# A low weight part of each up unit made by an accumulating transfer instead of VectorE, and the conditioning tiles dealt anew

## The chip, the core and the metric

The kernel runs on one core of a Trainium2 chip. A core has TensorE (PE in the profile; PEld is its weight load), VectorE (DVE), ScalarE (ACT), GpSimd (POOL) and SyncE (SP), which run their own instruction queues in order and wait for one another by semaphores, and 16 DMA engines that move data between the chip's memory and the tiles. The metric is the time of one execution in microseconds of device time. A ratio is time before over time after.

## The reference

A decoder trunk of four layers over 256 tokens of width 1024, in float32. The conditioning vector `c` gives six vectors of 1024 for each layer; each layer has a token mixer (layer 0 and 3: gMLP; 1: latent attention, MLA; 2: HGRN2) and a feed-forward part with a short convolution:

```python
for i in range(DEPTH):
    mod = c_act @ ada_w[i] + ada_b[i]
    sh1, sc1, g1, sh2, sc2, g2 = jnp.split(mod, 6, axis=-1)
    h = modulate(rmsnorm(x, mix_norm_g[i]), sh1, sc1)
    ...
    x = x + (1.0 + g1)[:, None, :] * y
    h = modulate(rmsnorm(x, ffn_norm_g[i]), sh2, sc2)
    x = x + (1.0 + g2)[:, None, :] * conv_ffn(h, ff_w_up[i], ff_conv_w[i], ff_conv_b[i], ff_w_down[i])
return rmsnorm(x, final_g)
```

`ada_w` is 4 x 1024 x 6144, `ff_w_up` 4 x 1024 x 5632 and `ff_w_down` 4 x 2816 x 1024. All of them are read once.

## The kernel before

**Weights in two parts.** Every product is made in a faster format that holds fewer bits (fp32r): a weight is split into a high part (the weight rounded to that format) and a low part (what is left), and so is the activation; three matmuls (high by high, high by low, low by high) replace one. The weights arrive in *units* of 128 x 2048 (1 MB) in a tile `raw`, of which there are five. A unit has two halves of 1024 columns. For each half, `conv_half` has ScalarE cast the high part `wh` (L214) and VectorE subtract it from `raw` to make the low part `wl` (L217); seven tiles of each go round. So 209 units give 418 casts and 418 subtractions.

**The order of units.** `want` writes all units into the list `plan` in the order of use. `unit` is called where a unit is used; it issues loads on SP's queue for units ahead (`dma_next`, L190) and converts units ahead, two or three beyond the one in use, then calls `pacing`.

**Stages.** In each layer: the mixer (gMLP: v, u and the output product go; MLA: cq, ckv, q, kn, heads, wo; HGRN2: hf, hq, hi, hg, o, wo), then the 22 units of the up projection (`ffn`: 48 matmuls a unit, then convolution and gate on ScalarE and VectorE, L1318 to L1325) and the 11 units of the down projection (dn). Between two stages stands a joint: `out_end` adds the product to `x` in pieces (L541, L542; the first piece is named `early` and is placed behind the last subtraction issued so far), forms the mean square, scales (`gx`, L477 to L481), and `modulated` turns `gx` by TensorE (`xt`, L489) and writes the next stage's activations in two parts (`hh`, `hlo`).

**Conditioning.** The 24 vectors of 1024 are the *conditioning units* (layer, part); the first two are made at the start. Each of the others has four tiles of 1 MB (named `adaw_part_tile`). Those in the list `ADA_P` are multiplied by TensorE (L331, into `adaps`; SP loads them at L317), those in `ADA_D` by VectorE (L356, two instructions of 1024 columns a tile; loaded at L347). Tables of numbers deal them out: `RATE` says how many tiles of each kind a unit of a stage loads, `GAPS` and `GAPRUN` how many TensorE tiles are held for and run in each of the joints, `MLA_ADA` and `HGF` at which places of MLA and HGRN2 one runs. Parts 2 and 5 are gates of the residual: `gate_row` clears a small tile `gcol` on GpSimd (L273), turns it on VectorE and stores it, and `gate_load` reads it back as `gx` (L293).

GpSimd has little else to do: fills, two broadcasts and a mask in each gMLP, and two products at the end.

Of the kernel before, what the change touches and what calls it, by code (L numbers as in the profile page):

```python
# [8 lines left out]
F32 = mybir.dt.float32  # L9
# [4 lines left out]
ALU = mybir.AluOpType  # L14
# [6 lines left out]
L = 4  # L21
# [3 lines left out]
NF = 22  # L25
GI = 2048
NRAW = 5
GAPS = [2, 4, 3, 3, 1, 2, 2, 0]
GAPRUN = [2, 2, 3, 3, 1, 2, 2]
GAPW = 7  # L30
GAPBIG = 3
LAST = 3
# [9 lines left out]
OLAG = 1  # L42
ROPE = 1
MLA_ADA = (2, 4, 6)
HGF = 2
HGO = "o0 o1 s0 a0 o2 s1 a1 n0 o3 s2 n1 w0 s3 n2 w1 n3 w2 w3"
HOLD = (3, 4)
ADA_P = [(0, 5), (1, 2), (1, 3), (2, 2), (2, 3), (2, 4), (3, 5)]
ADA_D = [(0, 2), (0, 3), (0, 4), (1, 0), (1, 1), (1, 4), (1, 5), (2, 0), (2, 1), (2, 5), (3, 0), (3, 1), (3, 2), (3, 3),
         (3, 4)]  # L50
RATE = {("mix", 0): (0.05, 0.9), ("u", 0): (0.1, 0.8), ("go", 0): (0.35, 0.6), ("up", 0): (0.1, 0.23),
        ("dn", 0): (0.0, 0.65), ("mix", 1): (2.0, 0.0), ("up", 1): (0.0, 0.2), ("dn", 1): (0.0, 0.85),
        ("mix", 2): (0.0, 0.0), ("lev", 2): (0.5, 0.0), ("hout", 2): (0.25, 0.0), ("up", 2): (0.0, 0.2),
        ("dn", 2): (0.0, 0.8), ("mix", 3): (0.0, 0.6), ("u", 3): (0.0, 0.5), ("go", 3): (0.0, 0.7),
        ("up", 3): (0.0, 0.0), ("dn", 3): (0.0, 0.0)}
MAGIC = 12582912.0
TWO_PI = 2.0 * math.pi
# [35 lines left out]
def build(ctx, tc, A, out, stages=None):  # L93
    nc = tc.nc
    pe, act, dve, pool = nc.tensor, nc.scalar, nc.vector, nc.gpsimd
# [60 lines left out]
    i = act.activation(cact[:], cin[:], AF.Silu)  # L156
# [12 lines left out]

    plan = []  # L170

    def want(aps):
        plan.extend(aps)

    state = {"dma": 0, "conv": 0, "use": 0, "ahead": 3, "chain": (), "behind": (), "manual": False, "left": 99, "tag": "raw", "p": 0.0, "d": 0.0, "gap": 0, "rate": {"p": 0.0, "d": 0.0}}
    raws = []
# [1 line left out]
    halves = []  # L178

    def dma_next():  # L180
        ap, n = plan[state["dma"]]
        raw = wp.tile([P, 2048], F32, tag="raw", name=f"raw{state['dma']}", bufs=NRAW)
        state["dma"] += 1
        if state["dma"] == 1:

            nc.sync.dma_start(raw[:, :1024], ap[:, :1024])
            raw_, ap = raw[:, 1024:], ap[:, 1024:]
        else:
            raw_ = raw[:, :n]
        i = nc.sync.dma_start(raw_, ap)  # L190
        state["lastdma"] = getattr(i, "ins", i)
        raws.append((raw, n))

    def conv_half():

        if not halves:
            if state["dma"] == state["conv"]:
                if state["dma"] == len(plan):
                    return
                dma_next()  # L200
            raw, n = raws.pop(0)
            ready.append([])
            halves.extend((raw, o, min(1024, n - o), state["conv"]) for o in range(0, n, 1024))
            state["conv"] += 1
        raw, o, w, n = halves.pop(0)
        wh = wp.tile([P, 1024], F32R, tag="wh", name=f"wh{n}_{o}", bufs=7)
        wl = wp.tile([P, 1024], F32R, tag="wl", name=f"wl{n}_{o}", bufs=7)
        with contextlib.ExitStack() as es:

            for ins in state["chain"]:  # L210
                es.enter_context(tc.issue_after(ins))
            if n == 0 and o and "first" in state:
                es.enter_context(tc.issue_after(state["first"][1]))
            act.copy(wh[:, :w], raw[:, o : o + w])  # L214
            if n == 0 and "first" in state:
                es.enter_context(tc.issue_after(state["first"][0]))
            i = dve.tensor_tensor(wl[:, :w], raw[:, o : o + w], wh[:, :w].bitcast(F32), op=ALU.subtract)  # L217
            state["sub"] = getattr(i, "ins", i)
        ready[-1].append((wh, wl))

    def unit(ahead=None, more=DMA_AHEAD):
# [11 lines left out]
    def pace(kind, l, left=None, tag=None):  # L233
        state["rate"] = dict(zip("pd", RATE[kind, l]))
        state["gap"] = GAPS[2 * l + (kind in ("up", "dn"))]
        if left is not None:
            state["left"] = left
        if tag is not None:
            state["tag"] = tag
# [67 lines left out]
    def ada_tile(name, shape):  # L307
        if state["tag"] == "big":
            return big(name, shape)
        return wp.tile(list(shape), F32, tag="raw", name=name, bufs=NRAW)  # L310

    def ada_tensor(l, u):


        def load(i):
            raw = ada_tile(f"adaw{l}_{u}_{i}", (P, 2, 4, 256))
            nc.sync.dma_start(raw[:].rearrange("p a b c -> p (a b c)"), A["adap"][ADA_P.index((l, u)), i])  # L317

            def run():
                h = ADA_P.index((l, u)) % 2  # L320
                ps = adaps[:, h, :]
                if i == 0 and pend[h] in late:
                    late.remove(pend[h])
                    pend[h][1]()
                with contextlib.ExitStack() as es:
                    for ins in state["behind"]:
                        es.enter_context(tc.issue_after(ins))
                    for k in range(2):
                        kc = 2 * i + k
                        for j in range(4):  # L330
                            pe.matmul(ps[32 * j : 32 * j + 32, :], crep(kc), raw[:, k, j, :], start=kc == 0, stop=kc == KC - 1,  # L331
                                      tile_position=(0, 32 * j))
                if i == 3:
                    pend[h] = (state["use"], lambda: mod_store(l, 8 * u, 8, ps), (l, u))
                    late.append(pend[h])
# [5 lines left out]
    def ada_vector(l, u):  # L341
# [3 lines left out]
        def load(i):  # L345
            raw = ada_tile(f"adaw{l}_{u}_{i}", (P, 2, D))
            nc.sync.dma_start(raw[:].rearrange("p a b -> p (a b)"), A["adad"][ADA_D.index((l, u)), i])  # L347

# [55 lines left out]
    def ada_run(m):  # L404
        if not loaded[m]:
            ada_load(m)
        if loaded[m]:
            loaded[m].pop(0)[1]()
            owner[m].pop(0)
# [57 lines left out]
    def root(t, sd):  # L467

        i = dve.reciprocal(sd[:, t : t + 1], sd[:, t : t + 1])
        state["chain"] = (getattr(i, "ins", i),)  # L470
        return sd[:, t : t + 1]

    def scaled(t, rs):

        xn = cur["gx"][:, t, :]
        if t == 0:
            dve.tensor_scalar_mul(xn, x[:, t, :], rs)  # L477
            return
        for o in (0, 256):
            dve.tensor_scalar_mul(xn[:, o : o + 256], x[:, t, o : o + 256], rs)  # L480
        i = act.activation(xn[:, 512:D], x[:, t, 512:D], AF.Copy, scale=rs)  # L481
        state["chain"] += (getattr(i, "ins", i),)
# [35 lines left out]
    def modulated(l, which):  # L518
# [4 lines left out]
        state["behind"] = (state["mm"],)  # L523
        for _ in loaded["p"][: GAPRUN[2 * l + which - 1]]:
            ada_run("p")
# [241 lines left out]
    def gmlp_units(j):  # L767
        want([(A["gmv"][j, i], 2048) for i in range(8)])
        want([(A["gmu"][j, i], 2048) for i in range(8)])
        want([(A["gmo"][j, i], 2048) for i in range(8)])  # L770
# [340 lines left out]
    def hgrn(l):  # L1111
# [176 lines left out]
        for step in HGO.split():  # L1288
            {"o": recur, "s": root, "n": normed, "w": wo.step, "a": lambda i: ada_run("p") if i < HGF else None}[step[0]](int(step[1]))

# [7 lines left out]
            nc.sync.dma_start(convs[l][:], A["cwb"][l])  # L1298

    def ffn_units(l):  # L1300
        want([(A["up"][l, i], 2048) for i in range(NF)])
        want([(A["dn"][l, i], 2048) for i in range(NF // 2)])

    def ffn(l):
        gh, gl = hilo("g", NF)
# [33 lines left out]
    for kind, l in stages:  # L1339
        if kind == "mix":  # L1340
            if l % 3 == 0:
                gmlp_units(l // 3)
            elif l == 1:
                mla_units()
            else:
                hg_units()
        elif kind == "ffn":
            ffn_units(l)
# [19 lines left out]
    for t in range(2):  # L1368
        act.activation(ss0[:, 6 + t : 7 + t], ss0[:, t : t + 1], AF.Sqrt, bias=epsc[:], scale=1.0 / D)
        scaled(t, root(t, ss0[:, 6:8]))  # L1370
    for m, units in (("p", ADA_P), ("d", ADA_D)):
        for l, u in units:
# [61 lines left out]
def pack(i):  # L1434
# [23 lines left out]
    def rng(a, n):  # L1458
# [12 lines left out]
    ap = aw.reshape(L, 4, 2, P, 6, 8, 4, 32)  # L1471
    r["adap"] = np.stack([ap[l, :, :, :, u].transpose(0, 2, 1, 4, 3, 5).reshape(4, P, 2048) for l, u in ADA_P])

    r["adad"] = np.stack([np.ascontiguousarray(aw[l, :, u * D : u * D + D].T).reshape(4, 2, P, D).transpose(0, 2, 1, 3).reshape(4, P, 2048)
                          for l, u in ADA_D])
    r["cb"] = np.ascontiguousarray(np.broadcast_to(f["c"], (P, D)))
# [48 lines left out]
```

## Time and profile before

| | |
|---|---|
| median of three runs (lowest, highest) | 1356.22 us (1356.13, 1357.68) |
| the profiled execution, its own time | 1358.56 us |
| its span in the profile | 1356.8 us |
| mean granted clock of TensorE | 0.991 |
| busy: TensorE, VectorE, ScalarE, GpSimd | 1320.5, 1129.1, 782.9, 20.0 us |
| moved by the DMA engines | 330.71 MB, mean 244 GB/s |

A line of a timeline has the start, the duration, the engine, the line of the kernel, the operation, what it writes and reads by the program's names, and in brackets how long the engine stood idle before it and what ended that. A line of a group has the count, the busy time and the mean in ns, then the idle time before its members. Matmuls overlap, so the time from one start to the next tells what one costs.

### The profile page before, as it was taken

What the parts mean: (1) busy time and instruction counts of PE and PEld (TensorE: products, weight loads), DVE (VectorE), ACT (ScalarE), POOL (GpSimd) and SP (SyncE); (2) the same over time, 40 slices, a digit from 0 to 9 for tenths busy, and PEclk for the clock granted to TensorE, in tenths of its full rate; (3) what the DMA queues carried; (4) which work ended last, traced back from release to release, by engine and by line L of the source; (5) the groups of instructions that cost most, each with busy time, mean ns of one, the idle gap of its engine ahead of it and who ended that gap; (6) DMA issues with size and microseconds to landing.
All of it is one profiled execution on the core that took longest, in us unless ns stands there. A gap on an engine that the chain in (4) does not pass through costs nothing. (4 is left out here: it accounts for less than half of the span.)

```text
span 1356.8 us, 25080 instructions
## 1 busy us (share of the span) xinstructions
PE 1320.5 (97%) x10197; PEld 1200.1 (88%) x10197; DVE 1129.1 (83%) x1865; ACT 782.9 (58%) x1230; POOL 20.0 (1%) x29
## 2 busy tenths in 40 slices
PE   9999999999979999999999999999999999999997
PEld 7799889997768799997897979999778998999986
DVE  5699979889776679999978967899988896888874
ACT  4664466665266566654585547666455753766642
POOL 0100000000000000000010000000001000000000
PEclk9999999999989999999999999999999999999999
DMA  9978955666985355579665364567968588355550
GB/s 380 357 266 312 397 205 214 257 218 232 394 325 203 125 187 202 200 303 372 249 221 199 109 261 156 187 217 280 372 255 338 198 326 330 122 172 178 198 198 32
DMA packets 49308, 330.71 MB, mean 244 GB/s; under 512 B 6565, under 2 KB 7717, under 8 KB 10407
## 3 DMA queue, kind: packets, MB, share of 16 engines
q1 hardware_dynamic: 48032, 326.95, 64.3%
q10 hardware_dynamic: 1160, 2.17, 0.5%
q8 instruction: 80, 1.31, 0.4%
q14 instruction: 36, 0.29, 0.1%
HBM read 328.01 MB, written 1.08 MB: 243 GB/s over the span
## 5 line engine op out<-in xcount | busy, mean ns | idle before, releaser
L214 ACT CAST wh<-raw 128x1024 fp32r<-128x1024 f32 x418 | 428.9, 1050 | 324.2 <-PE up L700 94.5
L217 DVE TENSOR_TENSOR wl<-raw,wh 128x1024 fp32r<-128x1024 f32 x418 | 506.9, 1231 | 93.4 <-ACT wh L214 88.7
L699 PE MATMUL up<-hh,wh 128*128 128x256 f32 x1280 | 314.3, 283 | 0.0
L700 PE MATMUL up<-hlo,wh 128*128 128x256 f32 x1280 | 314.1, 283 | 0.0
L699 PEld LDWEIGHTS up<-hh,wh 128*128 128x128 f32 x1280 | 245.7, 192 | 0.8 <-ACT gh L647 0.4
L700 PEld LDWEIGHTS up<-hlo,wh 128*128 128x128 f32 x1280 | 245.7, 192 | 0.0
L703 PE MATMUL up<-hh,wl 128*128 128x256 f32 x1280 | 179.7, 283 | 0.0
L703 PEld LDWEIGHTS up<-hh,wl 128*128 128x128 f32 x1280 | 165.1, 192 | 0.0
L356 DVE CUSTOM_DVE_ANT_0 adaw<-adaw,cbc,prm 128x1024 f32<-128x1024 f32 x120 | 151.3, 1280 | 3.9 <-DMA adaw<-adad 3.8
L1318 ACT ACTIVATE y<-up,cwb 128x256 f32<-128x256 f32 x176 | 98.8, 562 | 69.6 <-DVE y L1320 69.6
L248 PE MATMUL dn<-wl,gh 128*128 128x512 f32 x339 | 133.5, 394 | 1.5 <-DVE wl L217 1.5
L247 PE MATMUL dn<-wh,gh 128*128 128x512 f32 x339 | 130.2, 390 | 4.1 <-DVE y L1320 2.7
L249 PE MATMUL dn<-wh,gl 128*128 128x512 f32 x339 | 131.2, 390 | 0.0
L1319 DVE SCALAR_TENSOR_TENSOR y<-up,cwb,y 128x255 f32<-128x255 f32 x176 | 84.5, 480 | 29.8 <-ACT y L1318 29.0
L1320 DVE SCALAR_TENSOR_TENSOR y<-up,cwb,y 128x254 f32<-128x254 f32 x176 | 84.2, 478 | 1.8
L247 PEld LDWEIGHTS dn<-wh,gh 128*128 128x128 f32 x339 | 63.7, 188 | 18.5 <-ACT warm L624 3.5
L248 PEld LDWEIGHTS dn<-wl,gh 128*128 128x128 f32 x339 | 63.6, 188 | 18.4 <-DVE wl L217 5.7
L249 PEld LDWEIGHTS dn<-wh,gl 128*128 128x128 f32 x339 | 63.6, 188 | 12.8
L699 PE MATMUL u<-hh,wh 128*128 128x256 f32 x256 | 64.6, 290 | 0.0
L700 PE MATMUL u<-hlo,wh 128*128 128x256 f32 x256 | 62.8, 283 | 0.0
L648 DVE TENSOR_TENSOR gl<-g,gh 128x256 fp32r<-128x256 f32 x88 | 37.1, 421 | 19.3 <-ACT gh L647 18.0
L552 ACT ACTIVATE gated<-x 128x512 f32<-128x512 f32 (+1 forms) x40 | 21.8, 545 | 52.9 <-DVE x L542 50.4
(383 smaller groups left out, 2234.6 us busy)
## 6 DMA issues: line engine op xcount, KB each, us to landing
raw<-up SPq DMA_DIRECT2D x88, 1024.0 KB
adaw<-adad SPq DMA_DIRECT2D x60, 1024.0 KB
raw<-dn SPq DMA_DIRECT2D x44, 1024.0 KB
adaw<-adap SPq DMA_DIRECT2D x28, 1024.0 KB
raw<-gmu SPq DMA_DIRECT2D x16, 1024.0 KB
raw<-gmo SPq DMA_DIRECT2D x16, 1024.0 KB
raw<-gmv SPq DMA_DIRECT2D x15, 1024.0 KB
adaf<-ada SPq DMA_DIRECT2D x7, 1024.0 KB
```

The source lines that it names most:

```text
L214: act.copy(wh[:, :w], raw[:, o : o + w])
L217: i = dve.tensor_tensor(wl[:, :w], raw[:, o : o + w], wh[:, :w].bitcast(F32), op=ALU.subtract)
L247: pe.matmul(ps, lh, rh, start=start, stop=False)
L248: pe.matmul(ps, lh, rl, start=False, stop=False)
L249: i = pe.matmul(ps, ll, rh, start=False, stop=stop)
L356: r = dve.tensor_tensor_reduce(raw[:, e, :], raw[:, e, :], cbc[:], 1.0, prm[:, c0 : c0 + 1], ALU.mult, ALU.add, mod[:, l, b : b + 1])
L699: pe.matmul(ps[:, g, :], a, src_h(k), start=k == 0, stop=False)
L700: pe.matmul(ps[:, g, :], a, src_l(k), start=False, stop=False)
L703: i = pe.matmul(ps[:, g, :], b, src_h(k), start=False, stop=k == nk - 1)
L1318: act.activation(y[:], ps[:, e, :], AF.Identity, bias=b, scale=w[2])
L1319: dve.scalar_tensor_tensor(y[:, 1:], ps[:, e, : S - 1], w[1], y[:, 1:], op0=ALU.mult, op1=ALU.add)
L1320: dve.scalar_tensor_tensor(y[:, 2:], ps[:, e, : S - 2], w[0], y[:, 2:], op0=ALU.mult, op1=ALU.add)
```

## The change

`want` marks the units of which the first half is to be made in another way: all 22 up units and the first three dn units of each layer. For such a half ScalarE writes the negated, rounded weight into `wl` (`act.mul` by -1, which rounds as the cast does), and a transfer issued from GpSimd adds the weight from memory onto it, so that `wl` becomes the same difference. These bytes are read from memory a second time. The conditioning units are dealt anew: TensorE has six of them (24 tiles) where it had seven (28), VectorE 16 (64 tiles) where it had 15 (60); unit (0, 5) goes to VectorE, and the rates differ.

```diff
-GAPS = [2, 4, 3, 3, 1, 2, 2, 0]
-GAPRUN = [2, 2, 3, 3, 1, 2, 2]
+GAPS = [2, 4, 3, 3, 2, 2, 2, 0]
+GAPRUN = [2, 2, 3, 3, 2, 2, 2]
...
-HGF = 2
+HGF = 1
...
-ADA_P = [(0, 5), (1, 2), (1, 3), (2, 2), (2, 3), (2, 4), (3, 5)]
+ADA_P = [(1, 2), (1, 3), (1, 4), (2, 3), (2, 4), (3, 5)]
...
-RATE = {("mix", 0): (0.05, 0.9), ("u", 0): (0.1, 0.8), ("go", 0): (0.35, 0.6), ("up", 0): (0.1, 0.23),
-        ("dn", 0): (0.0, 0.65), ("mix", 1): (2.0, 0.0), ("up", 1): (0.0, 0.2), ("dn", 1): (0.0, 0.85),
+RATE = {("mix", 0): (0.05, 0.9), ("u", 0): (0.1, 0.85), ("go", 0): (0.35, 0.4), ("up", 0): (0.0, 0.34),
+        ("dn", 0): (0.0, 0.5), ("mix", 1): (2.0, 0.0), ("up", 1): (0.0, 0.36), ("dn", 1): (0.0, 0.9),
...
-    def want(aps):
-        plan.extend(aps)
+    def want(aps, again=0):
+
+        plan.extend((*a, i < again) for i, a in enumerate(aps))
...
+        again = plan[n][2] and o == 0
...
-            i = dve.tensor_tensor(wl[:, :w], raw[:, o : o + w], wh[:, :w].bitcast(F32), op=ALU.subtract)
-            state["sub"] = getattr(i, "ins", i)
+            if again:
+
+                act.mul(wl[:, :w], raw[:, o : o + w], -1.0)
+                pool.dma_start(wl[:, :w], plan[n][0][:, o : o + w], accum_op=ALU.add)
+            else:
+                i = dve.tensor_tensor(wl[:, :w], raw[:, o : o + w], wh[:, :w].bitcast(F32), op=ALU.subtract)
+                state["sub"] = getattr(i, "ins", i)
...
-        want([(A["up"][l, i], 2048) for i in range(NF)])
-        want([(A["dn"][l, i], 2048) for i in range(NF // 2)])
+        want([(A["up"][l, i], 2048) for i in range(NF)], NF)
+        want([(A["dn"][l, i], 2048) for i in range(NF // 2)], 3)
```

ScalarE's queue just before the joint into layer 0's up stage, where the first two up units are converted (`raw_1753` and `raw_1777` before, `raw_1751` and `raw_1773` now; the number in `wh_` or `wl_` is the half's first column). Before:

```order
L214 CAST wh_0_1781<-raw_1753 128x1024
L214 CAST wh_1024_1785<-raw_1753 128x1024
L214 CAST wh_0_1789<-raw_1777 128x1024
L214 CAST wh_1024_1793<-raw_1777 128x1024
L552 ACTIVATE gated,ss<-x 128x512 x2
```

And with the change:

```order
L215 CAST wh_0_1777<-raw_1751 128x1024
L220 ACTIVATE wl_0_1778<-raw_1751 128x1024
L215 CAST wh_1024_1782<-raw_1751 128x1024
L215 CAST wh_0_1786<-raw_1773 128x1024
L220 ACTIVATE wl_0_1787<-raw_1773 128x1024
L215 CAST wh_1024_1791<-raw_1773 128x1024
L558 ACTIVATE gated,ss<-x 128x512 x2
```

A copy of 1024 columns now stands between the casts of a unit's two halves, and VectorE's subtraction of the second half, behind which `early` is placed, waits for the second cast.

SP's queue in the second half of layer 0's down stage, from the load of the gate to the first units of MLA (`adad` are VectorE's conditioning tiles, `adap` TensorE's). Before:

```order
L293 DMA gx<-gate_3381 128x1024
L190 DMA raw_3843<-dn 128x2048
L190 DMA raw_3881<-dn 128x2048
L317 DMA adaw_2_3_3893<-adap 128x2048
L347 DMA adaw_1_2_3628<-adad 128x2048
L347 DMA adaw_1_3_3700<-adad 128x2048
L347 DMA adaw_4_0_3736<-adad 128x2048
L317 DMA adaw_2_0_3775<-adap 128x2048
L347 DMA adaw_4_1_3813<-adad 128x2048
L317 DMA adaw_2_1_3815<-adap 128x2048
L347 DMA adaw_4_2_3853<-adad 128x2048
L317 DMA adaw_2_2_3855<-adap 128x2048
```

Behind these came one dn unit, `adaw_4_3_3931` and the two units of mla_a. With the change, from the same place:

```order
L299 DMA gx<-gate_2865 128x1024
L190 DMA raw_3848<-dn 128x2048
L353 DMA adaw_1_0_3672<-adad 128x2048
L353 DMA adaw_1_1_3744<-adad 128x2048
L323 DMA adaw_2_2_3780<-adap 128x2048
L353 DMA adaw_1_2_3818<-adad 128x2048
L323 DMA adaw_2_3_3820<-adap 128x2048
L323 DMA adaw_3_0_3858<-adap 128x2048
L190 DMA raw_3884<-dn 128x2048
L353 DMA adaw_1_3_3896<-adad 128x2048
L323 DMA adaw_3_1_3898<-adap 128x2048
```

Behind these come one dn unit and the two units of mla_a: 13 tiles of 1 MB from the load of the gate on, where there were 15.

More of the change, by code (lines that the diff above doesn't have):

```diff
@@ L44 @@
 MLA_ADA = (2, 4, 6)
-HGF = 2
+HGF = 1
 HGO = "o0 o1 s0 a0 o2 s1 a1 n0 o3 s2 n1 w0 s3 n2 w1 n3 w2 w3"
 HOLD = (3, 4)
-ADA_P = [(0, 5), (1, 2), (1, 3), (2, 2), (2, 3), (2, 4), (3, 5)]
-ADA_D = [(0, 2), (0, 3), (0, 4), (1, 0), (1, 1), (1, 4), (1, 5), (2, 0), (2, 1), (2, 5), (3, 0), (3, 1), (3, 2), (3, 3),
-         (3, 4)]
-RATE = {("mix", 0): (0.05, 0.9), ("u", 0): (0.1, 0.8), ("go", 0): (0.35, 0.6), ("up", 0): (0.1, 0.23),
-        ("dn", 0): (0.0, 0.65), ("mix", 1): (2.0, 0.0), ("up", 1): (0.0, 0.2), ("dn", 1): (0.0, 0.85),
-        ("mix", 2): (0.0, 0.0), ("lev", 2): (0.5, 0.0), ("hout", 2): (0.25, 0.0), ("up", 2): (0.0, 0.2),
-        ("dn", 2): (0.0, 0.8), ("mix", 3): (0.0, 0.6), ("u", 3): (0.0, 0.5), ("go", 3): (0.0, 0.7),
+ADA_P = [(1, 2), (1, 3), (1, 4), (2, 3), (2, 4), (3, 5)]
+ADA_D = [(l, u) for l in range(L) for u in range(6) if (l, u) > (0, 1) and (l, u) not in ADA_P]
+RATE = {("mix", 0): (0.05, 0.9), ("u", 0): (0.1, 0.85), ("go", 0): (0.35, 0.4), ("up", 0): (0.0, 0.34),
+        ("dn", 0): (0.0, 0.5), ("mix", 1): (2.0, 0.0), ("up", 1): (0.0, 0.36), ("dn", 1): (0.0, 0.9),
+        ("mix", 2): (0.0, 0.0), ("lev", 2): (0.5, 0.0), ("hout", 2): (0.0, 0.0), ("up", 2): (0.0, 0.36),
+        ("dn", 2): (0.0, 0.6), ("mix", 3): (0.0, 0.5), ("u", 3): (0.0, 0.5), ("go", 3): (0.0, 0.5),
         ("up", 3): (0.0, 0.0), ("dn", 3): (0.0, 0.0)}
@@ L180, in dma_next @@
     def dma_next():
-        ap, n = plan[state["dma"]]
+        ap, n, _ = plan[state["dma"]]
         raw = wp.tile([P, 2048], F32, tag="raw", name=f"raw{state['dma']}", bufs=NRAW)
```

## The prediction

> **What bounds the kernel now.** I read the page's head, then stretches by stage, then the timeline at the joints between stages.
>
> ```profile
> span 1356.8 us, 25080 instructions
> PE 1320.5 (97%) x10197; PEld 1200.1 (88%) x10197; DVE 1129.1 (83%) x1865; ACT 782.9 (58%) x1230; POOL 20.0 (1%) x29
> ...
> L214 ACT CAST wh<-raw 128x1024 fp32r<-128x1024 f32 x418 | 428.9, 1050 | 324.2 <-PE up L700 94.5
> L217 DVE TENSOR_TENSOR wl<-raw,wh 128x1024 fp32r<-128x1024 f32 x418 | 506.9, 1231 | 93.4 <-ACT wh L214 88.7
> ...
> L356 DVE CUSTOM_DVE_ANT_0 adaw<-adaw,cbc,prm 128x1024 f32<-128x1024 f32 x120 | 151.3, 1280 | 3.9 <-DMA adaw<-adad 3.8
> ```
>
> PE is at work nearly always, so an engine that gets less to do gives time back only where PE stands. The stretches show where that is (the columns are the stretch, its length, busy us of PE, PEld, DVE, ACT and POOL, granted clock, DMA share, GB/s). The first row is the down projection of layer 0, the next the up projection of layer 1, then the down projection of layer 1 and the up projection of layer 3.
>
> ```profile
> 307.50:370.00 62.50, 59.59 (x258) 47.54 (x257) 53.13 (x85) 25.87 (x33) 0.00 (x0) 1.00 0.83 328
> 475.00:601.70 126.70, 126.70 (x1059) 126.70 (x1057) 110.96 (x191) 82.36 (x131) 0.26 (x2) 1.00 0.61 222
> 601.70:662.00 60.30, 58.94 (x259) 47.72 (x259) 56.93 (x81) 25.33 (x33) 0.00 (x0) 1.00 0.92 363
> ...
> 1162.00:1288.00 126.00, 126.00 (x1053) 126.00 (x1052) 103.93 (x180) 82.46 (x133) 0.12 (x1) 1.00 0.50 172
> ```
>
> **An up stage is PE alone**: 126.70 of 126.70 us, while DVE has 110.96 (88%) and ACT 82.36 (65%). Nothing that relieves DVE there shortens it. What can be won lies at the joints, and the worst one stands between the down projection of layer 0 and layer 1's attention:
>
> ```profile
> 361.75 1.99 ACT L214 CAST wh<-raw 128x1024 fp32r<-128x1024 f32 x2 [16.14 <-DMA raw<-dn]
> 366.70 2.00 ACT L214 CAST wh<-raw 128x1024 fp32r<-128x1024 f32 x2 [2.96 <-DMA raw<-mla_a]
> 367.79 4.80 DVE L217 TENSOR_TENSOR wl<-raw,wh 128x1024 fp32r<-128x1024 f32 x4
> 369.14 2.00 ACT L214 CAST wh<-raw 128x1024 fp32r<-128x1024 f32 x2 [0.44 <-DMA raw<-mla_a]
> 372.50 0.68 DVE L541 TENSOR_TENSOR early<-dn,gx 128x512 f32<-128x512 f32 x1
> 381.06 3.71 PE L489 MATMUL xt<-ident,gx 128*128 128x128 f32 x16 [6.94 <-DVE gx L477]
> 384.42 0.56 PE L687 MATMUL cq<-hh,wh 128*128 128x256 f32 x1
> ```
>
> ACT waits 16.14 us for the last tiles of dn, then for those of mla_a; DVE makes their low parts, and only behind these stands the residual ("early", 372.50), from which the chain to the next transposes takes 8.56 us. PE has ended its tail by then. So the joint hangs on the transfers, and they are saturated:
>
> ```profile
> 171.40:174.90 3.50, 0.35 (x9) 0.09 (x2) 3.25 (x11) 2.34 (x9) 0.00 (x0) 1.00 0.94 393
> 373.70:381.00 7.30, 0.41 (x8) 0.00 (x0) 6.82 (x17) 4.73 (x13) 0.00 (x0) 0.71 1.01 425
> 381.00:388.00 7.00, 6.94 (x36) 6.75 (x36) 6.06 (x17) 6.64 (x12) 0.00 (x0) 0.57 0.96 386
> 741.70:744.20 2.50, 0.21 (x27) 0.11 (x13) 2.50 (x4) 1.72 (x2) 0.00 (x0) 1.00 0.18 26
> 744.20:749.00 4.80, 4.80 (x80) 4.11 (x80) 4.69 (x6) 0.00 (x0) 0.00 (x0) 0.64 0.90 323
> ```
>
> 425 GB/s at a full share is the most that the engines move here. PE idles for 7.30 us, and in the 7.00 us after it the granted clock is 0.57. The joint into layer 0's up stage (first row) is a smaller case of the same.
>
> **The change, part by part.** *The low parts.* 100 halves (22 up units and 3 dn units in each of four layers) leave L217: 100 x 1.231 = 123 us off DVE. ACT gets 100 scaled copies; the row nearest is its cast of the same shape, so 100 x 1.05 = 105 us. One DVE unit of conditioning is added, 8 x 1.28 = 10 us. In the stretch of layer 1's up stage DVE goes from 110.96 by -21 x 1.23 and, with four tiles more, +8 x 1.28 to about 95 of 126.7; ACT from 82.36 by +22 x 1.05 to about 105 (83%). Neither becomes the bound, and PE stays where it is: **0 us in the up stages**. PE's 5.76 us a unit hide it (126.7/22), with units converted two ahead, so a low part may land some 11 us after its copy. If that cover is gone, each unit is late by what the slowest engine exceeds 5.76 us.
>
> *The accumulating transfer* is in no row of before. Bounds: below, it costs its 0.52 MB at 420 GB/s, 1.25 us of all engines; above, that its bytes are read from memory, read from the tile and written back, three times as much, 3.75 us. Layer 1's up stage moves 222 x 126.7 = 28.1 MB now; the four tiles more make 32.3, and engines at 420 GB/s could move 53.2. So 20.9 MB, or 0.95 MB for each of 22 accumulates, is free: they are hidden up to 2.26 us apiece, 1.8 times the plain price. I take 1.25 to 2.2 us, nearest to the only rows there are, plain loads, and hence nothing for it. On GpSimd's queue stand behind such a transfer the next one and the fills of "gcol" (eight in all, on whose landing DVE waits); each waits for ACT's copy at most, and DVE's own next subtraction is behind the same copies, so I cost them at 0, at most 1 us each.
>
> The Trainium skill, *DMA: Bandwidth & Descriptors* (Specifications), puts the limit of memory to one core near 358 GB/s. By that, accumulates would be hidden only up to about 1.4 us (an estimate). The trace disagrees, with its 425 GB/s.
>
> *Layer 0's down stage.* On SP's queue, from the load of gx to the second tile of mla_a, stand 15 tiles of 1 MB before and 13 now, two conditioning tiles fewer. At 425 GB/s a tile is 2.5 us: the chain from 366.70 on starts 5.0 us earlier. What is late next is DVE's chain itself, which begins then at 367.5, before the tail ends. PE's 7.30 us of idling fall to about 2.3, and with them the slow clock: 0.43 x 7.00 = 3.0 us, of which I take 2.5, since ACT and DVE are busy there too. Together **-7.5 us**; at worst the room is filled by other transfers, 0. In the stage itself PE idles 62.50 - 59.59 = 2.91 us against 60.30 - 58.94 = 1.36 in layer 1's, because of the same late tiles: **-1.5 us** (0 at worst).
>
> *Conditioning tiles on PE* go from 28 to 24. Two stood in layer 0's up stage:
>
> ```profile
> 223.78 0.88 PE L703 MATMUL up<-hh,wl 128*128 128x256 f32 x6
> 224.59 1.07 PE L331 MATMUL adaps<-adaw,cact 128*32 128x256 f32 x16
> 225.59 0.39 PE L699 MATMUL up<-hh,wh 128*128 128x256 f32 x1
> ```
>
> The next up matmul would have started 0.72 us after 223.78 and starts at 225.59: 1.09 us a tile, **-2.2 us**. One fewer stands in HGRN, where PE also waits for others: **-0.5 us** (0 to -1.1). Two are gone from the joint into layer 3's up stage, where nothing else fills PE:
>
> ```profile
> 1157.18 0.28 PE L249 MATMUL tail<-wh,yl 128*128 128x256 f32 x1
> 1157.39 1.93 PE L331 MATMUL adaps<-adaw,cact 128*32 128x256 f32 x32
> 1159.84 0.63 PE L489 MATMUL xt<-ident,gx 128*128 128x128 f32 x4 [0.52 <-DVE ss L469]
> ```
>
> PE stands there 2.5 us now. After the 2.50 us at 741.70 the clock was 0.64 for 4.80 us, 1.7 us lost; so 0 to +1.7, and I take **+0.9 us**. The Trainium skill, *TensorE: Matmul & The Clock Gate* (Part 1), has the clock halved after an idle window of about 3.4 us; by it this term is 0. The row at 741.70 differs.
>
> *Layer 1's down stage* gets one tile more on SP's queue (2.5 us) and three accumulates (3.75 us) into a stretch whose engines have 8% of 60.30 us free, 4.8 us: **+1.5 us** at its joint (0 to +5).
>
> *The joint into layer 0's up stage:*
>
> ```profile
> 163.09 2.00 ACT L214 CAST wh<-raw 128x1024 fp32r<-128x1024 f32 x2 [0.42 <-DMA raw<-up]
> ...
> 166.46 0.68 DVE L541 TENSOR_TENSOR early<-go,gx 128x512 f32<-128x512 f32 x1
> ```
>
> One tile less makes the last up tile land 2.5 us earlier; the accumulate of the unit ahead takes 1.25 of it back, and the scaled copy that stands before the second cast 1.05. Sum **-0.2 us**; bounds -4 (all DVE waits gone and the clock kept) and +2.3 (the accumulate at its upper price).
>
> Sum: -7.5 - 1.5 - 2.2 - 0.5 + 0.9 + 1.5 - 0.2 = **-9.5 us**. The profiled execution took 1358.56 us, 1.8 more than its span; it becomes 1349.1. The median of the three runs is 1356.22, 2.3 under it, so I forecast 1356.2 - 9.5 = **1347 us**.
>
> **Rivals.** *The transfers become the bound of the up stages* (slower). It decides from 2.26 us an accumulate. At 3.1 us, the middle of the range above that, each of the 66 units of layers 0 to 2 is 0.84 us late, +55 us, and layer 3, at 172 GB/s now, has room for it: 1356 + 55 - 9 = 1402; just past the point, at 2.45 us, it is +12, and the time is 1359. For it speaks that such a transfer must read its target as well; against it, that all four stages show 0.50 to 0.61 of the engines used.
>
> *The room in layer 0's down stage is filled* (no change): the accumulates of the three dn units and what the up stage left over take the two tiles' place. Then only the tiles on PE count, -2.7 + 2.4, and the time is about 1356. The full share at 373.70 speaks for it; against it, that ACT's 16.14 us of waiting begin long after these three units.
>
> *DVE's relief is worth more*: SP's loads also wait for buffers that DVE's subtractions free, so with less behind DVE the down stages begin with more loaded, and the joint into layer 0's up stage gains its 4 us too: 1340.
>
> That the change doesn't do what it says would show as DVE's L217 group still at 418; the order of instructions excludes that.
>
> **How the numbers follow.** Forecast (with the sum's own bounds, 1343 to 1353) 0.45; more relief, 0.25; no change, 0.12; transfers bound, 0.18. A measurement of this kernel can tell about 0.2%, 2.7 us, from no change. Faster takes the first two cases, 0.70; same 0.12; slower 0.18. The range from 1336 to 1366 holds the first three and the mild end of the last; left out are the fully bound up stages and a gain beyond 20 us.
>
> **What would show it.** Right: the stretch of layer 1's up stage still 126.7 us with PE busy throughout, DMA share between 0.8 and 1.0; "early" in layer 0's down stage at least 4 us ahead of the tail's end and the granted clock 1.00 after it; no tiles inside layer 0's up stage. Wrong: PE waiting for low parts made by GpSimd's transfer inside an up stage, a DMA share of 1.0 there, or ACT above 95% of such a stretch. If "early" still waits for tiles of mla_a, the main term has failed.

## The result and the profile after

The changed kernel takes **1371.69 us** (median of five runs, 1366.64 us the lowest), and the kernel before, run five times beside it, 1357.68 us. Every ratio from here on is time after over time before, so that a number above 1 means slower: 1.0094, with a 95% interval of 1.0072 to 1.0116. One of the five runs took 1823.44 us, at a granted clock of 0.654 where the others had 0.988 to 0.993, and is left out of the ratio; the median of the other four is 1370.57 us. The forecast was 1347 us with a range of 1336 to 1366. The change makes the kernel about 0.9% slower, and both the sign and the range were wrong.

The page of the changed kernel (its profiled execution took 1369.45 us), first the head, the queue that GpSimd issues to (packets, MB, share of 16 engines' span), then the groups:

```profile
span 1367.7 us, 25279 instructions
PE 1315.2 (96%) x10133; PEld 1196.8 (88%) x10133; DVE 1038.8 (76%) x1779; ACT 870.8 (64%) x1330; POOL 111.3 (8%) x129
...
q0 software_dynamic: 14400, 52.44, 19.8%
...
L223 DVE TENSOR_TENSOR wl<-raw,wh 128x1024 fp32r<-128x1024 f32 x318 | 388.2, 1236 | 130.8 <-ACT wh L215 130.1
...
L709 PE MATMUL up<-hh,wl 128*128 128x256 f32 x1280 | 180.8, 284 | 9.9 <-DMA wl<-up 9.9
L362 DVE CUSTOM_DVE_ANT_0 adaw<-adaw,cbc,prm 128x1024 f32<-128x1024 f32 x128 | 164.0, 1292 | 20.3 <-DMA adaw<-adad 20.3
...
L253 PE MATMUL dn<-wh,gh 128*128 128x512 f32 x339 | 134.0, 395 | 13.9 <-DVE y L1326 13.9
...
L220 ACT ACTIVATE wl<-raw 128x1024 fp32r<-128x1024 f32 x100 | 105.5, 1055 | 5.8 <-PE wo L254 2.9
...
wl<-up POOLq DMA_DIRECT2D x88, 512.0 KB, 10.4
```

The change does what it says: the subtractions fall from 418 to 318, and DVE is 90 us less busy. PE's own work is 5 us less too. Still the span is 10.9 us longer, so PE waits more. One wait is new, PE's 9.9 us for low parts made by GpSimd's transfers. Two have grown: DVE's for conditioning tiles to 20.3 us (3.9 before) and PE's in the down stages, for "y" from DVE, to 13.9 us. The row of before for the latter has 2.7:

```profile
L247 PE MATMUL dn<-wh,gh 128*128 128x512 f32 x339 | 130.2, 390 | 4.1 <-DVE y L1320 2.7
```

The first row to read is q0's. The packets of its 100 transfers took 19.8% of 16 engines over 1367.7 us, so **one accumulating transfer takes 0.198 x 1367.7 / 100 = 2.71 us of all engines** for 0.52 MB. The break-even in the prediction was 2.26 us.

The stretches of the changed kernel, with the columns of the prediction's rows (stretch, length, busy us of PE, PEld, DVE, ACT, POOL, granted clock, DMA share, GB/s): the joint behind layer 0's down stage and what follows it, then layer 1's up stage, its down stage, and the start of that down stage.

```profile
464.20:595.30 131.10, 127.18 (x1052) 126.24 (x1051) 96.84 (x184) 99.91 (x154) 18.39 (x22) 1.00 0.97 293
595.30:660.20 64.90, 59.50 (x259) 48.94 (x259) 56.56 (x81) 29.01 (x36) 1.74 (x2) 0.97 1.01 405
```

```profile
370.80:373.30 2.50, 0.42 (x9) 0.03 (x1) 2.14 (x8) 2.04 (x9) 0.00 (x0) 1.00 1.01 426
373.30:380.00 6.70, 6.68 (x56) 6.44 (x56) 5.92 (x16) 6.62 (x12) 0.12 (x1) 1.00 1.01 428
...
604.40:612.00 7.60, 7.60 (x27) 6.13 (x28) 7.60 (x15) 2.77 (x5) 0.00 (x0) 0.79 1.03 332
```

In layer 1's up stage the DMA engines are full (0.97, before 0.61) although only 293 GB/s are moved. The bytes of an accumulating transfer are counted once (52.44 MB for 100), and the engines work on it for longer. At the joint behind layer 0's down stage the intended gain is there: PE idles 2.45 us instead of 7.30, and the granted clock stays at 1.00 where it had been 0.57. The timeline of the changed kernel shows where that gain is lost again, at the end of layer 1's up stage:

```profile
588.83 1.28 DVE L362 CUSTOM_DVE_ANT_0 adaw<-adaw,cbc,prm 128x1024 f32<-128x1024 f32 x1 [5.90 <-DMA adaw<-adad]
...
590.55 0.56 ACT L1324 ACTIVATE y<-up,cwb 128x256 f32<-128x256 f32 x1 [7.26 <-DVE y L1326]
...
598.61 0.39 PE L255 MATMUL dn<-wh,gl 128*128 128x512 f32 x1
604.40 0.77 PE L253 MATMUL dn<-wh,gh 128*128 128x512 f32 x1 [5.40 <-DVE y L1326]
```

DVE stands 5.90 us for a conditioning tile that comes late through the full engines. Behind it in DVE's queue stands the convolution of the up stage's last units, ACT stands 7.26 us for that, and PE, which has run out of activations, stands from 598.61 to 604.40 in the down stage, after which the clock is 0.79 for 7.60 us. Layer 2 repeats it, in another stretch of the same timeline, with PE standing for 6.79 us from 952.66 on:

```profile
943.61 1.28 DVE L362 CUSTOM_DVE_ANT_0 adaw<-adaw,cbc,prm 128x1024 f32<-128x1024 f32 x1 [6.80 <-DMA adaw<-adad]
```

So a good part of the loss is not where the transfer itself is waited for, but one engine and one stage further on.

### The profile page after: what moved, and what is told of

It reads as the page before. It is cut to its first block, busy times and chain, and to the rows that moved or that the text cites. A ratio compares the mean times of both kernels' runs of the same rounds, so it can differ in the third digit from the quotient of the medians.

```text
span 1367.7 us, 25279 instructions
## 1 busy us (share of the span) xinstructions
PE 1315.2 (96%) x10133; PEld 1196.8 (88%) x10133; DVE 1038.8 (76%) x1779; ACT 870.8 (64%) x1330; POOL 111.3 (8%) x129
## 3 DMA queue, kind: packets, MB, share of 16 engines
q0 software_dynamic: 14400, 52.44, 19.8%
## 4 chain that ended last, share of the span: by engine, by line
PE 55%; DVE 17%; DMA 13%; issue 7%; ACT 6%; POOL 0%; SPq 0%; ACTq 0%; DVEq 0%; POOLq 0%
PE dn L253 5%; PE dn L255 4%; PE dn L254 4%; PE up L709 4%; PE up L706 4%; PE up L705 4%; DVE wl L223 4%; DVE adaw L362 4%; DMA adaw<-adad 3%; DMA wl<-up 3%; ACT wh L215 2%; DMA raw<-dn 2%; PE v L750 2%; DMA adaf<-ada 1%; DVE x L548 1%
## 5 line engine op out<-in xcount | busy, mean ns | idle before, releaser
L223 DVE TENSOR_TENSOR wl<-raw,wh 128x1024 fp32r<-128x1024 f32 x318 | 388.2, 1236 | 130.8 <-ACT wh L215 130.1
L362 DVE CUSTOM_DVE_ANT_0 adaw<-adaw,cbc,prm 128x1024 f32<-128x1024 f32 x128 | 164.0, 1292 | 20.3 <-DMA adaw<-adad 20.3
L709 PEld LDWEIGHTS up<-hh,wl 128*128 128x128 f32 x1280 | 164.9, 192 | 12.3 <-DMA wl<-up 12.2
L253 PE MATMUL dn<-wh,gh 128*128 128x512 f32 x339 | 134.0, 395 | 13.9 <-DVE y L1326 13.9
L221 POOL DMA_DIRECT2D wl<-up x88 | 76.8, 873 | 767.5 <-ACT wl L220 407.3
L220 ACT ACTIVATE wl<-raw 128x1024 fp32r<-128x1024 f32 x100 | 105.5, 1055 | 5.8 <-PE wo L254 2.9
## 6 DMA issues: line engine op xcount, KB each, us to landing
wl<-up POOLq DMA_DIRECT2D x88, 512.0 KB, 10.4
```

What stands on the lines that cost most here:

```text
L220: act.mul(wl[:, :w], raw[:, o : o + w], -1.0)
L253: pe.matmul(ps, lh, rh, start=start, stop=False)
L362: r = dve.tensor_tensor_reduce(raw[:, e, :], raw[:, e, :], cbc[:], 1.0, prm[:, c0 : c0 + 1], ALU.mult, ALU.add, mod[:, l, b : b + 1])
L709: i = pe.matmul(ps[:, g, :], b, src_h(k), start=False, stop=k == nk - 1)
```

## The experiments

The table has the time, the ratio, and four lengths worked out from the starts of PE's matmuls in each trace: the up stages of layers 0, 1 and 2 (first to last up matmul) and the down stages of layers 1 and 2 (from there to the last matmul of the tail). The last column is PE's wait for transferred low parts of up units, by the list of waits. Each ratio is against runs of the kernel before made beside that kernel; their medians lie between 1357.41 and 1358.23 us.

| kernel | us | ratio (95%) | up 0 | up 1 | up 2 | down 1 | down 2 | PE waits |
|---|---|---|---|---|---|---|---|---|
| before | 1357.68 | 1 | 129.4 | 126.7 | 126.7 | 62.2 | 62.2 | 0 |
| after | 1371.69 | 1.0094 (1.0072, 1.0116) | 129.9 | 131.0 | 130.7 | 67.2 | 68.5 | 9.9 |
| e1: old deal, all accumulates | 1357.02 | 1.0001 (0.9988, 1.0015) | 131.7 | 128.1 | 128.7 | 61.9 | 61.7 | 4.5 |
| e2: new deal, no accumulates | 1359.49 | 1.0015 (1.0005, 1.0024) | 126.7 | 126.7 | 126.7 | 65.5 | 65.5 | 0 |
| e3: transfers as plain loads | 1339.92 | 0.9873 (0.9859, 0.9888) | 126.7 | 128.2 | 130.6 | 60.0 | 60.0 | 3.4 |
| e4: copies without transfers | 1336.52 | 0.9844 (0.9828, 0.9861) | 126.7 | 126.7 | 126.7 | 60.0 | 60.0 | 0 |
| e5: every second unit | 1385.44 | 1.0211 (1.0186, 1.0235) | 137.2 | 142.3 | 139.5 | 61.0 | 61.0 | 25.7 |
| e6: every third unit | 1425.84 | 1.0494 (1.0469, 1.0518) | 144.6 | 148.2 | 148.0 | 64.1 | 64.2 | 47.3 |
| e7: e5 with the old deal | 1362.71 | 1.0027 (1.0011, 1.0044) | 130.7 | 131.7 | 133.8 | 60.0 | 60.9 | 8.8 |
| e8: e5, copies early | 1353.22 | 0.9953 (0.9935, 0.9971) | 128.3 | 128.2 | 128.6 | 61.6 | 61.6 | 3.5 |
| e9: after, copies early | 1365.65 | 1.0051 (1.0031, 1.0071) | 128.8 | 128.0 | 128.2 | 70.1 | 70.8 | 3.8 |
| e10: two units of three, early | 1341.17 | 0.9872 (0.9856, 0.9889) | 127.5 | 128.9 | 127.6 | 60.0 | 60.0 | 2.8 |
| e11: e10 with the old deal | 1349.25 | 0.9937 (0.9921, 0.9953) | 130.6 | 127.7 | 126.7 | 60.1 | 60.1 | 1.4 |
| e12: e6, copies early | 1367.02 | 1.0069 (1.0047, 1.009) | 129.4 | 132.4 | 129.8 | 62.9 | 63.0 | 7.6 |

The expectations name four theories: A, the DMA engines are the bound; B, ScalarE's copies delay its queue; C, the tiles dealt to VectorE are the loss; D, the path over GpSimd is too long for units converted two ahead. The later "engines" is A, "latency" is D, and "order" is new: the copy is issued too late.

**The two halves of the change, each alone.** e1 puts all 100 accumulates into the kernel before and leaves its deal; e2 has the new deal and makes all low parts by subtraction. In `ffn_units` of e2:

```diff
-        want([(A["up"][l, i], 2048) for i in range(NF)], NF)
-        want([(A["dn"][l, i], 2048) for i in range(NF // 2)], 3)
+        want([(A["up"][l, i], 2048) for i in range(NF)])
+        want([(A["dn"][l, i], 2048) for i in range(NF // 2)])
```

> The accumulating transfers with the deal of before (tables, rates and lists of before). Theory A (the transfer engines are the bound: an accumulate holds them for about 2.7 us, from its queue's 19.8% of the span over 100 transfers): layer 1's up stage needs 28.1 MB / 420 GB/s = 67 us and 22 x 2.7 = 59 us, 126 of 126.7, just full, so PE waits under 2 us in each up stage instead of 2 to 4, the stall at the start of layer 1's and 2's down stages falls from 5.8 and 6.8 us to 2 or 3; the joint after layer 0's down stage stays as late as before (12 us); time 1355 to 1364. Theory B (ScalarE's extra copies delay its queue) and theory D (the path over GpSimd takes 10 us whatever is moved, too long for two units ahead): the up stages lose as much as with the whole change, time 1368 or more. Theory C (the tiles dealt to VectorE are the loss): as fast as before or faster, 1350 to 1357.

> The new deal of conditioning tiles without accumulating transfers: VectorE makes every low part again. Theory A: the transfers in the up stages stay under 70% share, PE never waits for a low part in an up stage; but VectorE then has 5.22 + 0.36 x 2.73 = 6.2 us a unit in the up stages of layers 1 and 2 for 5.76 us of PE, so it falls behind by up to 10 us a stage, which shows as waits on VectorE (not on a transfer) late in the stage and in dn; the joint after layer 0's down stage keeps its gain of 6 us; time 1350 to 1368. Theory C: the whole loss stays, 1368 or more, with the same waits on transfers. B and D: 1350 or less.

e1 is level with before, e2 0.15% slower, with down stages 3.3 us longer in layers 1 and 2. Neither half by itself makes the loss of 0.94%: it needs both, the accumulates and, in the same up stages, more conditioning tiles. Theory C falls. (The new deal differs in more than unit (0, 5): by its diff unit (2, 2) goes to VectorE as well, and (1, 4) to TensorE.)

**The transfer made cheaper, and taken away.** e3 loads the weight over the negated copy instead of adding to it, which puts the weight itself in the place of its low part, with the same queue, bytes read and place behind the copy. e4 leaves the transfer out, and the low part is then the negated copy alone.

```diff
-                pool.dma_start(wl[:, :w], plan[n][0][:, o : o + w], accum_op=ALU.add)
+                pool.dma_start(wl[:, :w], plan[n][0][:, o : o + w])
```

> The change with its 100 transfers as plain loads of the same bytes from the same queue (the low parts then hold the weights themselves, so the output is another). Theory A: such a load holds the engines for 1.25 to 1.5 us, half of an accumulate; the share of the up stages falls to 0.8, PE waits nowhere in an up stage, the stalls at the start of the down stages go back to 1.7 us; time 1345 to 1352. Theories B, C and D: no change against the whole change, 1367 to 1371.

> The change without its 100 transfers: ScalarE's negated copies stay and are used as the low parts (the weights' low parts are left out of the output). Theory A: share of the up stages about 0.65, PE waits nowhere in an up stage, time 1343 to 1350. Theory B: up stages as with the whole change, 1367 to 1371. Theory C: the same, 1367 or more. Theory D: 1343 to 1350.

The queue of e3, layer 1's up stage of e3, and layer 1's up and down stages of e4:

```profile
q0 software_dynamic: 14400, 52.44, 11.4%
```

```profile
450.00:580.00 130.00, 128.07 (x1083) 125.57 (x1076) 102.37 (x200) 105.41 (x164) 11.76 (x23) 1.00 0.84 310
```

```profile
450.00:577.00 127.00, 126.27 (x1070) 123.79 (x1069) 102.08 (x200) 103.38 (x162) 0.13 (x1) 1.00 0.64 237
577.00:637.00 60.00, 60.00 (x295) 50.90 (x295) 51.86 (x73) 28.82 (x35) 0.00 (x0) 1.00 0.88 353
```

A plain load of the same 52.44 MB takes 0.114 x 1338.1 / 100 = 1.53 us of the engines, an accumulate 2.71 us, 1.8 times as much. Making the transfer plain is worth 32 us (1371.69 against 1339.92). It shortens the landing too, from 10.4 to 7.6 us (medians), and e3 doesn't part the two; e9 below tells more. (One wait of PE for a low part, 2.2 us, lengthens e3's up 2.) Theories B and D fall, by which e3 would have stayed at 1367 us or more. Without transfers the rest of the change, copies on ScalarE and the deal, gains 21 us (e4), and in layers 0 to 2 ScalarE's copies hide wholly in the up stages. Both kernels came out faster than theory A's own ranges, by 5 and 6.5 us. The engines' account for layer 1, up and down together, agrees with A to 4 us. By e4 the stages need 0.64 x 127 + 0.88 x 60 = 134 us of the engines' 187 without transfers (0.88 is their share in e4's down stage). 25 accumulates at 2.71 us add 68, so 202 are needed and 15 are late; measured are 198.2 us for the two stages in the changed kernel and 186.7 in e4, 11.5 late.

**Fewer accumulates.** By that account every second or every third unit should fit easily. The change in e5, in the new deal (e6 has `range(2, NF, 3)`, e7 the selection of e5 in the deal before; `want` takes the units in place of a count):

```diff
-        want([(A["up"][l, i], 2048) for i in range(NF)], NF)
-        want([(A["dn"][l, i], 2048) for i in range(NF // 2)], 3)
+        want([(A["up"][l, i], 2048) for i in range(NF)], range(1, NF, 2) if l < LAST else ())
+        want([(A["dn"][l, i], 2048) for i in range(NF // 2)])
```

> The whole change's deal, with an accumulating transfer for every second up unit of layers 0 to 2 alone (33 instead of 100; none in layer 3's up stage and none in dn). Theory A: layer 1's up stage needs 32 MB / 420 GB/s = 77 us and 11 x 2.7 = 30 us of the engines, 107 of 126.7, so PE waits nowhere for a low part; VectorE has 5.2 + 1.0 - 0.6 = 5.6 us a unit for 5.76 of PE, so it does not fall behind; the joint after layer 0's down stage keeps its gain; time 1338 to 1347, faster than both kernels. A theory by which each such transfer costs its share of the loss (33 of 100 of the 10 us between the new deal without and with them): 1362.

> The same with every third up unit of layers 0 to 2 (seven a stage, 21 in all). Theory A: the engines have 96 of 126.7 us, VectorE 5.2 + 1.0 - 0.4 = 5.8 us a unit and falls behind by a little; time 1342 to 1352, between every second unit and none (1359.5). By a share of the loss for each: 1361.

> Every second up unit of layers 0 to 2 by an accumulating transfer, with the deal of before. Theory A: no waits in the up stages, engines at 28.1 MB / 420 GB/s + 30 = 97 of 126.7 us; what remains is the late joint after layer 0's down stage, whose queue still holds 15 tiles: time 1348 to 1356, slower than with the new deal by the 6 to 8 us of that joint and the two tiles on TensorE in layer 0's up stage.

All three missed, e5 and e6 by far: from every unit to every third, **the fewer accumulates, the slower**. The engines are not the cause of that. The stretch of e6's layer 1 up stage has a share of 0.66 with PE at work for 130 of 148 us:

```profile
483.00:631.00 148.00, 130.47 (x1066) 126.78 (x1066) 110.50 (x202) 88.27 (x141) 6.22 (x8) 0.97 0.66 216
```

The timelines of e6 at the end of that stage, of ACT, of GpSimd and of PE, show a second mechanism:

```profile
596.13 1.05 ACT L215 CAST wh<-raw 128x1024 fp32r<-128x1024 f32 x1
...
599.00 1.04 ACT L215 CAST wh<-raw 128x1024 fp32r<-128x1024 f32 x1 [1.06 <-PE up L706]
...
605.15 1.05 ACT L215 CAST wh<-raw 128x1024 fp32r<-128x1024 f32 x1 [4.34 <-PE up L706]
...
608.03 1.05 ACT L215 CAST wh<-raw 128x1024 fp32r<-128x1024 f32 x1 [1.06 <-PE up L706]
...
610.91 1.05 ACT L215 CAST wh<-raw 128x1024 fp32r<-128x1024 f32 x1 [1.07 <-PE up L706]
...
613.79 1.05 ACT L215 CAST wh<-raw 128x1024 fp32r<-128x1024 f32 x1 [1.06 <-PE up L706]
614.75 1.05 ACT L220 ACTIVATE wl<-raw 128x1024 fp32r<-128x1024 f32 x1
```

```profile
616.20 0.86 POOL L221 DMA_DIRECT2D wl<-up  x1 [19.68 <-ACT wl L220]
```

```profile
627.27 1.43 PE L709 MATMUL up<-hh,wl 128*128 128x256 f32 x5 [7.76 <-DMA wl<-up]
```

By the program's order the first of these casts is that of unit 20's first half, and the copy at 614.75 belongs to the same half. Between them the scheduler put five more casts, of the second half, of unit 21 and of the first dn unit, and each of those waits for a buffer of high parts that PE must free. So the copy runs 17.6 us after it could have, the transfer is issued at 616.20, needs 10.6 us to land, and PE stands until 627.27. As long as PE stands it frees no buffer, and the next copy is late as well. In e6, PE used 18 of the 21 accumulated low parts within 0.6 us of their landing; the other three are the first of each stage. In layer 1's up stage the mean time from the end of a half's cast to its copy, worked out from ACT's records, is 1.9 us in e1, 2.9 in the changed kernel, 4.7 in e7, 7.3 in e5 and 10.4 in e6, and the longer up stages of e5 against e7, with the same units taken, go with it. Why the scheduler places the copies later in one kernel than in the other is not shown.

**The copy brought forward.** e8, e9 and e12 are e5, the whole change and e6 with the next half's cast bound behind the scaled copy, and nothing else; e10 has the same and takes the units 1, 2, 4, 5 and so on of layers 0 to 2, e11 is e10 with the deal before.

```diff
+            if "neg" in state:
+                es.enter_context(tc.issue_after(state["neg"]))
             act.copy(wh[:, :w], raw[:, o : o + w])
...
-                act.mul(wl[:, :w], raw[:, o : o + w], -1.0)
+                i = act.mul(wl[:, :w], raw[:, o : o + w], -1.0)
+                state["neg"] = getattr(i, "ins", i)
```

> As e5 (the new deal, accumulates for the odd up units of layers 0 to 2), and each scaled copy is now bound to stand on ScalarE ahead of the next half's cast. In e5 it stood behind two later casts, which wait for buffers that PE frees, so PE used the low part only 9.6 us after the copy, against 8.7 us that the transfer takes to land. Theory order (the copy is issued too late): the lead becomes 14 to 17 us, PE's waits for the low parts go, the up stages of layers 0 to 2 fall from 137 to 142 us back to 126.7 to 128.5, and the time from 1385 to between 1337 and 1346. Engines' need in layer 1's up stage: 0.64 x 126.7 = 81 us without transfers (e4) + 11 x 2.71 = 111 of 126.7, so the bound on the engines allows it. Theory latency (the path over GpSimd is too long for two units ahead in any order): the up stages stay above 132 us and the time above 1365.

> The whole change, with each scaled copy bound ahead of the next half's cast. Theory engines: need in layer 1's up stage is 81 + 22 x 2.71 = 141 us of 126.7, so 10 us or more are still late in each of layers 1 and 2, partly in the down stages behind them; the order gives back little, and the time stays between 1355 and 1372, with a DMA share of 0.95 or more in the up stages. Theory order: the late copies were the whole loss, and the time falls to between 1337 and 1347.

> As e8 with accumulates for two up units of three in layers 0 to 2 (units 1, 2, 4, 5 and so on). Theories engines and order together: need in layer 1's up stage 81 + 14 x 2.71 = 119 us of 126.7, just within, so the time is 1338 to 1352 and the DMA share 0.93 or so; if landings lengthen at that share, some waits come back, and it lies above e8. Theory latency: above 1370.

> As e10 (accumulates for two up units of three in layers 0 to 2, each scaled copy bound ahead of the next cast), but with the conditioning tiles dealt as in the kernel before. If the new deal brings nothing by itself but only uses the time that DVE is given (e2, the deal alone, was 1359.5), this kernel keeps the long joint behind layer 0's down stage (10 to 12 us against 6.2 or less) and the tiles on PE, and takes 1347 to 1355. If the relief of DVE alone is the gain and the deal nothing, it takes 1339 to 1344, as e10.

> As e6, the slowest of all (1425.84: accumulates for units 2, 5, 8 and so on of layers 0 to 2, new deal), with each scaled copy bound ahead of the next half's cast. Theory order: the up stages fall from 144.6, 148.2 and 148.0 us to between 126.7 and 129, and the time to 1351 to 1361 (DVE is relieved less than in e8, 1353; the deal alone is 1359.5). Theory that a lone transfer is slow of itself (latency): the up stages stay above 135.

The order of one copy is worth 32 us in e5 (to e8) and 59 us in e6 (to e12). PE's waits for low parts fall from 25.7 to 3.5 us and from 47.3 to 7.6. The theory that the path over GpSimd is too long in any order falls. e8's up stages came out as expected; its time missed by 7 us. The joint behind layer 0's down stage idles 5.48 us there (gap between PE's starts at 367.69 and 373.17) where e10's idles 1.69; I put that down to DVE, which has 385 subtractions left in e8 and 376 in e10, but nothing was run to show it. e12 missed by 6 us: no cast stands between a half's cast and its copy now, yet the copy still comes 5.8 us behind in the mean of layer 1's up stage, since ACT waits for DVE's convolution and gate (3.65 us before 576.94, ahead of the copy at 579.01; 397 subtractions are left on DVE), and the up stages stay 3 to 6 us too long.

e9 shows the bound that remains in the whole change. Its stretches of layer 1, up and down:

```profile
460.00:588.00 128.00, 126.38 (x1057) 125.18 (x1055) 92.34 (x177) 95.16 (x145) 18.39 (x22) 1.00 0.95 291
588.00:658.00 70.00, 62.75 (x280) 51.43 (x279) 60.95 (x89) 33.50 (x43) 1.73 (x2) 0.95 1.00 390
```

With the copies early the up stage is nearly whole again and PE waits 3.8 us in all for transferred low parts, and what is late moves into the down stage, at a share of 1.00: 198 us for both, as in the changed kernel. DVE's wait is there still:

```profile
586.50 1.28 DVE L365 CUSTOM_DVE_ANT_0 adaw<-adaw,cbc,prm 128x1024 f32<-128x1024 f32 x1 [6.73 <-DMA adaw<-adad]
```

The order gives back about 0.4% (6 us), the engines keep the rest. e10 takes away 58 of the 100 accumulates and needs 134 + 14 x 2.71 = 172 us of 187. Its layer 1, up and down:

```profile
460.00:589.00 129.00, 127.07 (x1054) 126.61 (x1053) 110.34 (x202) 96.29 (x149) 11.42 (x14) 1.00 0.92 301
589.00:649.00 60.00, 60.00 (x293) 49.66 (x295) 55.67 (x80) 25.52 (x35) 0.00 (x0) 1.00 0.90 355
```

PE is busy for all of the 60.00 us of the down stage, and **e10, at 1341.17 us, beats both kernels**: 1.3% under before. It is 4.7 us above e4, which has no transfers at all.

e11 tells what the deal is worth: 8 us (1349.25 against 1341.17) once DVE is relieved, while by itself (e2) it costs 2. At the joint behind layer 0's down stage PE idles 7.30 us before, 5.84 with the deal alone, 4.53 with the relief alone (e11), 1.69 with both (e10).

## Why the prediction was wrong, point by point

**The step that failed** is "I take 1.25 to 2.2 us, nearest to the only rows there are, plain loads, and hence nothing for it". An accumulate takes 2.71 us of the engines. The prediction's own bounds were 1.25 and 3.75 us, and its own threshold, 2.26 us, lay near their middle (the middle of what lies above it is 3.0, not the 3.1 that the rival used). Taking the lower part because the nearest rows were plain loads put 0 in the sum and 0.18 on the rival, where the bounds alone allowed more than half. The rival, *the transfers become the bound of the up stages*, named the mechanism, and with the measured price its own formula gives 66 x (2.71 - 2.26) = 30 us and 1356 + 30 - 9 = 1377, 5 above the result. That it comes so near is in part luck, for the threshold was too high: it divides bytes by 420 GB/s, but the row of layer 1's up stage has 222 GB/s at a share of 0.61, which is 364 GB/s at a full one. By e4's share the stage has (127 - 81) / 22 = 2.1 us for each accumulate, and by that the formula gives some 40 us. Its place was not quite right: the lateness shows partly in the up stages (+4.4 and +4.0 us in layers 1 and 2, +1.9 in layer 3, 126.7 to 128.6) and more in the down stages behind them (+5.0 and +6.3), by way of late conditioning tiles on DVE's queue.

**The cover in the up stages.** That "a low part may land some 11 us after its copy" was too thin a cover to cost at nothing. Transfers land 10.4 us after issue (median), and the mean from a copy's end to PE's use is 12.3 to 12.7 us in layers 0 to 2 without the first two units of each stage, worked out from the records of copies and matmuls. The prediction took the copy to run beside its unit's casts. Where it runs is decided by the scheduler, and in e5 and e6 that decided the time. In the changed kernel itself it is the smaller part: e9, with the copies early, has 1.0051 against 1.0094, 6 us, where the plain transfers of e3 give 32.

**DVE and ACT** do not become the bound, as forecast: 96.84 and 99.91 us busy in layer 1's up stage (about 95 and 105 were expected), and e4's up stages are 126.7.

**Layer 0's down stage**, -7.5 us: the size was right. The stretch from layer 0's last tail matmul to the end of layer 1's attention went from 97.3 to 89.3 us, with 2.45 us of idling (2.3 forecast) and the clock kept. "Early" runs at 364.72, 4.3 us ahead of the last tail matmul (369.05). The reason was half right: I put it on two tiles fewer in SP's queue, but of the idling the deal alone takes off 1.5 us (e2) and DVE's relief alone 1.9 (e1) to 2.8 (e11); only the two together take off 4.9 and more, so that the size owes something to luck. In the stage itself -1.5 was forecast and -1.7 measured.

**Tiles on PE**, -2.2 us in layer 0's up stage: e2 and e4 have 2.7 us less there (129.4 to 126.7). In the changed kernel waits for low parts use it up (129.9). Of HGRN2's -0.5 nothing shows: from layer 1's last tail matmul to layer 2's first up matmul it is 155.9 us in both kernels.

**Layer 1's down stage**, +1.5: mis-sized, +5.0. With the measured price its own sum, 2.5 + 3 x 2.71 - 4.8, is 5.8. Layer 2's, +6.3, was in no term at all.

**The joints** into the up stages: layer 0's -1.5 us (forecast -0.2), layer 3's 0 (forecast +0.9). There PE idles 2.66 us, and the clock behind it is whole:

```profile
1166.70:1169.00 2.30, 0.00 (x0) 0.01 (x1) 2.08 (x9) 1.47 (x7) 0.00 (x0) 1.00 0.03 11
1169.00:1174.00 5.00, 4.98 (x43) 4.97 (x44) 4.20 (x11) 4.92 (x10) 0.00 (x0) 1.00 0.00 0
```

The Trainium skill, *TensorE: Matmul & The Clock Gate* (Part 1), has the clock halved after an idle window of about 3.4 us, and this joint agrees with it. The row of before from which I took the slow clock (0.64 after 2.50 us) does not carry over to this joint, and no run here explains it.

**More relief**, the rival at 1340, is about what the change would have been with free transfers: e4 takes 1336.5. My -9.5 us for all but the transfers was too small by half; e4 gains 21.

## What to carry to other kernels

Price an operation that the profile does not show by the whole of its bounds, and where the break-even lies inside them, give the loss its share of the chance. An accumulating transfer is not a plain load of the same bytes (2.71 against 1.53 us here): look at the share of the DMA engines in the stage, not at GB/s, and count what the stage can still take before choosing how many to issue. And a step that starts a long path (copy, issue, landing) has to stand early in its engine's in-order queue; if a scheduler places it, look where, since the wait then shows on another engine.

## What the runs showed of the hardware that was not expected

An accumulating transfer of 0.52 MB took 2.71 us of all 16 engines by the time of its packets (2.71 in e1 as well: 20.0% of 1355.2 us over 100), a plain one issued from the same queue 1.53. The figure is no constant: in the kernels with 21 to 42 of them it is 2.8 to 3.1 us (4.2% of 1420.4 us over 21 in e6, 4.8% of 1365.7 us over 21 in e12). That the reading of the target makes the difference was not tried by itself.

Such a transfer lands late even where the engines are not full: 8.7 us after issue (median in e6, with the engines at 0.66 in layer 1's up stage), 10.4 in the changed kernel, 7.6 for the plain load in e3.

The Trainium skill, *DMA: Bandwidth & Descriptors* (Anatomy of one DMA, on the path of GpSimd), fits about 2.0 us and the bytes over 436 GB/s for one transfer, 3.2 us here (an estimate). Beside the other loads of these kernels no run agrees: the plain transfers of e3 land 3.9 us after issue at the shortest, 7.6 in the median.
